# Up projection of an encoder block: hi-hi and hi-lo matmuls joined into one of 512 columns, relu squared on ScalarE, a weight sum by DMA

## The chip, the cores and the metric

The kernel runs on one core of a Trainium2 chip. The metric is the device time of one execution in microseconds (us). One execution of it was also taken with the hardware profiler; all rows below are from that one.

## The reference

One layer of an encoder block over 512 tokens of width 2048, all in float32:

```
h = rmsnorm(x) ; p = h @ w_in                      # 2048 x 6144
mix = concat(8 differential heads, 8 neighbourhood heads)
x = x + mix @ w_out
u = rmsnorm(x) @ w_up                              # 512 x 2048 @ 2048 x 8192
x = x + square(relu(u)) @ w_down                   # 8192 x 2048
y = rmsnorm(x)
```

The change is in the product with `w_up` and in the relu squared behind it.

## The kernel before

TensorE multiplies tiles of type float32r. To keep float32 accuracy each operand is split in two: a high part (a cast on ScalarE, L94, to a tile `wh`) and the rest (a subtraction on VectorE, L95, to a tile `wl`). A product of two split operands is three matmuls: high by high, high by low, low by high.

The up projection cuts its matrices in halves both ways and uses Strassen-like sums, in the Winograd form: seven products in the place of eight. Seven sums of blocks of the activations (`a11`, `a12`, `s2`, `s1_`, `s3`, `s4`, `a22`; each split, each with its high and low part side by side in one tile) are made once. The loop `for q in range(32)` then takes 256 columns of `w_up` a turn. Its four weight blocks (128 x 1024 each, 512 KB) are loaded by the SP queue into the pool `rx` (6 buffers), in the order b11, b12, b22, b21. The generator `quad` makes from them the seven weight operands, in this order: b11, b21, t2 = t1 + b22, t1 = b11 + b12, t3 = b12 + b22, b22, t4 = t2 + b21. The sums are VectorE additions (L471) into the pool tag `raw` (3 buffers); each operand is split into a `wh` and a `wl` tile, and each of these two tags has three buffers. This work is queued with raised priority, some way ahead of the products. The activations are the moving side (256 tokens), the weights the stationary one.

`prod` (L593) runs one product: 8 k-tiles by 3 matmuls of 256 columns, 24 matmuls. Three PSUM banks hold the results of a turn: pU gets a11, then s2, s3 and a22 on top of it; pV gets a12; pW gets s1_, then s4. Between the products that add to pU or pW the value so far is taken out: ScalarE keeps copies p1 (after a11), u2 (after s2) and p5 (after s1_), and VectorE combines them with later values into four quarters of a tile `c` (L605, L611, L613; the fourth is a ScalarE copy, L615). A product that adds to a bank waits for the copy that reads it. L617 makes relu squared of the whole of `c` in one VectorE pass, and GpSimd's queue writes it to DRAM (`ud`), from where the down projection (L776) reads it.

The order of the instructions on each engine is set when the program is built, by a list scheduler with priorities; at run time every engine takes its own instructions strictly in that order. A tile of a pool is given out again when its last reader is done.

The down projection already has transfers that add to a tile in SBUF (L681, `accum_op=ALU.add`), issued by GpSimd's queue.

Of the kernel before, what the change touches and what calls it, by code (L numbers as in the profile page):

```python
# [9 lines left out]
F32 = mybir.dt.float32  # L10
F32R = mybir.dt.float32r
AF = mybir.ActivationFunctionType
ALU = mybir.AluOpType
AX = mybir.AxisListType

P = 128
# [19 lines left out]
def hymba_kernel(ctx: ExitStack, tc: tile.TileContext, x, x_t, norm_mix_g, w_dq, w_dk, w_dv, w_nq, w_nk, w_nv, lams,  # L36
                 subln_g, rel_bias, w_out, norm_mlp_g, w_up, w_down, norm_final_g, cos_t, sin_t, mask_t, out):
    nc = tc.nc
# [54 lines left out]
    def split(hi, lo, src, eng=None):  # L93
        nc.scalar.copy(out=hi, in_=src)  # L94
        (eng or nc.vector).tensor_sub(out=lo, in0=src, in1=hi.bitcast(F32))  # L95
# [55 lines left out]
    with tc.tile_pool(name="start", bufs=4) as sp, tc.high_priority(offset=20000):  # L151
        acc = sp.tile([P, 2 * SEQ], F32, name="acc", bufs=1)
        xs = []
        for u in range(4):
# [8 lines left out]
            for k in range(4):  # L163
# [3 lines left out]
                                               op0=ALU.mult, op1=ALU.subtract)  # L167
# [14 lines left out]
        for t in range(NT):  # L182
            nc.tensor.matmul(out=ssx[:, t:t + 1], lhsT=acc[:, t * P:(t + 1) * P], rhs=ones_f[:, 0:1],
                             start=True, stop=True)
# [11 lines left out]
    with es:  # L196
# [19 lines left out]
        with tc.issue_after(last_sq.ins):  # L216
            for r in range(GH):
                src = bass.AP(rel_bias.tensor, rel_bias.offset + 15 * 15 + 7 - r, [[TD * 15, NH], [-15, 16], [1, TRUN]])
# [187 lines left out]
        for hp in range(NH // 2):  # L406
# [5 lines left out]
            last = hp == NH // 2 - 1  # L412
# [14 lines left out]
    stage = up_es.enter_context(tc.tile_pool(name="stage", bufs=2))  # L427
# [34 lines left out]
    def quad(src, pool_t):  # L462

        with tc.high_priority(offset=3000):
            b11, b12, b22, b21 = (rx.tile([P, 1024], F32, name="b", tag="b") for _ in range(4))
            for t, i in ((b11, 0), (b12, 1), (b22, 3), (b21, 2)):
                nc.sync.dma_start(out=t, in_=src[i])

            def add(a, b):
                t = pool_t.tile([P, 1024], F32, name="ts", tag="raw")  # L470
                nc.vector.tensor_add(out=t, in0=a, in1=b)  # L471
                return t

            def parts(t):
                h = wpool.tile([P, 1024], F32R, name="wh", tag="wh")
                l = wpool.tile([P, 1024], F32R, name="wl", tag="wl")
                split(h, l, t)
                return h.rearrange("p (k c) -> p k c", k=8), l.rearrange("p (k c) -> p k c", k=8)

            t1 = add(b11, b12)  # L480
            yield parts(b11)
            t2 = add(t1, b22)
            yield parts(b21)
            yield parts(t2)
            yield parts(t1)
            t3 = add(b12, b22)
            yield parts(t3)
            yield parts(b22)
            t4 = add(t2, b21)
            yield parts(t4)  # L490
# [8 lines left out]
    with tc.tile_pool(name="trans", bufs=2) as tr:  # L499
        for n in range(4):  # L500
# [7 lines left out]
            for u in range(8):  # L508
# [3 lines left out]
                for t in range(NT):  # L512
                    ts = slice(t * P, (t + 1) * P)
                    for k in range(2):
                        kt = 2 * u + k
                        m = mixT[kt // 4]
# [10 lines left out]
            for th in range(2):  # L527
# [3 lines left out]
                for t in (2 * th, 2 * th + 1):  # L531
                    xt = tr.tile([P, 512], F32, name="xg", tag="xg", bufs=3)
                    nc.vector.scalar_tensor_tensor(out=xt, in0=xb[t], scalar=s1[:, t:t + 1], in1=gM, op0=ALU.mult,
                                                   op1=ALU.mult)
                    xg.append(xt)
                for k2 in range(2):
                    pt = ((psa,) * 4, (psb, psc) * 2)[n % 2][2 * th + k2]().rearrange("p (k t) -> p k t", k=2)
                    for k in range(2):
                        for i in range(2):
                            nc.tensor.transpose(out=pt[:, k, i * P:(i + 1) * P],  # L540
                                                in_=xg[i][:, (2 * k2 + k) * P:(2 * k2 + k + 1) * P], identity=ident)
# [13 lines left out]
    def psm():  # L555
        return psM.tile([P, 512], F32, name="pm", tag="pm")
# [27 lines left out]

    for q in range(32):
        ops = quad(w_up[q], wpool)
        pU, pV, pW = (psm()[:, :256] for _ in range(3))

        def prod(ps, s, first, last):
            th_, tl_ = next(ops)  # L590
            for k in range(8):
                for i, (a, j) in enumerate(((th_, 0), (th_, 1), (tl_, 0))):
                    nc.tensor.matmul(out=ps, lhsT=a[:, k], rhs=s[k // 4][:, j, k % 4], start=first and k + i == 0,  # L593
                                     stop=last and k == 7 and i == 2, skip_group_check=True)

        def keep_copy(ps, name):
            t = stage.tile([P, 256], F32, name=name, tag=name)
            nc.scalar.copy(out=t, in_=ps)  # L598
            return t

        c = stage.tile([P, 2, 2, 256], F32, name="c", tag="c")
        prod(pU, a11, True, True)
        p1 = keep_copy(pU, "p1")
        prod(pV, a12, True, True)
        nc.vector.tensor_add(out=c[:, 0, 0], in0=pV, in1=p1)  # L605
        prod(pU, s2, False, True)
        u2 = keep_copy(pU, "u2")
        prod(pW, s1_, True, True)
        p5 = keep_copy(pW, "p5")
        prod(pU, s3, False, True)  # L610
        nc.vector.scalar_tensor_tensor(out=c[:, 1, 1], in0=pU, scalar=-1.0, in1=p5, op0=ALU.mult, op1=ALU.subtract)  # L611
        prod(pW, s4, False, True)
        nc.vector.scalar_tensor_tensor(out=c[:, 1, 0], in0=pW, scalar=-1.0, in1=u2, op0=ALU.mult, op1=ALU.subtract)  # L613
        prod(pU, a22, False, True)
        nc.scalar.copy(out=c[:, 0, 1], in_=pU)  # L615
        cf = c.rearrange("p m h t -> p (m h t)")
        nc.vector.scalar_tensor_tensor(out=cf, in0=cf, scalar=0.0, in1=cf, op0=ALU.max, op1=ALU.mult)  # L617
        nc.gpsimd.dma_start(out=ud[q], in_=cf)


# [184 lines left out]
    for p in range(16):  # L805
        c, n = divmod(p, 2)
        o = chunks[c]
        pU, pW = X[p % 2], X[1 - p % 2]
        end = p == 15
# [36 lines left out]
        for b in range(2):  # L846
            t = 2 + b
# [3 lines left out]
                                           op1=ALU.add)  # L851
# [87 lines left out]
```

## Time and profile before

| | |
|---|---|
| median of 3 runs | 2127.74 us (2125.85 to 2128.14) |
| the profiled execution | 2128.14 us; span from first to last instruction 2126.0 us |
| busy: TensorE matmuls | 2080.7 us (98%), 12604 matmuls |
| busy: weight loads of TensorE | 1853.7 us (87%) |
| busy: VectorE, ScalarE, GpSimd | 1527.0 us (72%), 982.5 us (46%), 282.6 us (13%) |
| granted clock of TensorE, mean | 0.993 of full speed |
| up projection, L593 | 5376 matmuls between 841.7 and 1482.7 us |

Matmuls overlap one another, so the length shown for one is not its cost; the distance between the starts of two is. A row of the timeline is: start in us, length in us, engine, line, operation, output <- inputs, shape, count, and in brackets the idle time before it with what ended it. Names are the program's without buffer numbers: `pm` is any of the three banks, `a` any of a11, a12 and a22, `s` any of s2, s3 and s4 (s1_ shows as s__7304), `p` is p1 or p5, `ts` any of t1 to t4.

### The profile page before, as it was taken

What the parts mean: (1) busy time and instruction counts of PE and PEld (TensorE: products, weight loads), DVE (VectorE), ACT (ScalarE), POOL (GpSimd) and SP (SyncE); (2) the same over time, 40 slices, a digit from 0 to 9 for tenths busy, and PEclk for the clock granted to TensorE, in tenths of its full rate; (3) what the DMA queues carried; (4) which work ended last, traced back from release to release, by engine and by line L of the source; (5) the groups of instructions that cost most, each with busy time, mean ns of one, the idle gap of its engine ahead of it and who ended that gap; (6) DMA issues with size and microseconds to landing.
All of it is one profiled execution on the core that took longest, in us unless ns stands there. A gap on an engine that the chain in (4) does not pass through costs nothing.

```text
span 2126.0 us, 31142 instructions
## 1 busy us (share of the span) xinstructions
PE 2080.7 (98%) x12604; PEld 1853.7 (87%) x12604; DVE 1527.0 (72%) x1707; ACT 982.5 (46%) x1342; POOL 282.6 (13%) x271
## 2 busy tenths in 40 slices
PE   7999999999999999999999999999999999999996
PEld 6989989989888887999999999999888878788875
DVE  6656556556566345877777877778777788788788
ACT  5444444444445434444444444444554555445544
POOL 5221221221221000000000000000011111111110
PEclk8999999999999999999999999999999999999998
DMA  6322332332324642634334434335888798798873
GB/s 217 114 95 89 109 97 88 108 98 85 105 92 136 223 156 87 209 129 149 129 119 150 141 128 139 131 129 178 226 223 216 178 243 217 190 246 211 214 182 109
DMA packets 109552, 323.51 MB, mean 152 GB/s; under 512 B 11296, under 2 KB 27872, under 8 KB 109408
## 3 DMA queue, kind: packets, MB, share of 16 engines
q1 hardware_dynamic: 83040, 241.33, 34.0%
q0 software_dynamic: 25936, 79.65, 16.7%
q8 instruction: 99, 1.62, 0.3%
q10 hardware_dynamic: 432, 0.53, 0.1%
q14 instruction: 45, 0.37, 0.1%
HBM read 275.33 MB, written 30.25 MB: 144 GB/s over the span
## 4 chain that ended last, share of the span: by engine, by line
PE 81%; DVE 8%; DMA 5%; issue 2%; ACT 2%; POOL 0%; SPq 0%; ACTq 0%; DVEq 0%; POOLq 0%
PE pm L593 28%; PE x L776 13%; PE pa L141 8%; PE pa L98 7%; PE pa L99 7%; PE pa L100 7%; DMA b<-in_w_down 5%; DVE wl L95 3%; PE v L776 2%; PE pb L99 1%; PE pb L98 1%; PE pb L100 1%; DVE b L685 1%; PE pc L98 1%; PE pc L99 1%
## 5 line engine op out<-in xcount | busy, mean ns | idle before, releaser
L94 ACT CAST wh<-b 128x1024 fp32r<-128x1024 f32 x320 | 333.3, 1049 | 452.9 <-PE x L776 156.2
L776 PE MATMUL x<-wh,uT 128*128 128x512 f32 x1536 | 482.0, 392 | 8.7 <-DVE y L790 7.8
L95 DVE TENSOR_TENSOR wl<-b,wh 128x1024 fp32r<-128x1024 f32 x320 | 388.3, 1220 | 115.8 <-ACT wh L94 114.2
L776 PEld LDWEIGHTS x<-wh,uT 128*128 128x128 f32 x1536 | 288.8, 188 | 76.5 <-issue 4.5
L776 PE MATMUL x<-wl,uT 128*128 128x512 f32 x768 | 301.2, 392 | 0.9 <-DVE wl L95 0.9
L593 PE MATMUL pm<-s,wh 128*128 128x256 f32 x1536 | 280.2, 283 | 3.4 <-ACT p L598 2.3
L593 PE MATMUL pm<-a,wh 128*128 128x256 f32 x1536 | 267.3, 279 | 2.0 <-DVE c L611 1.4
L593 PEld LDWEIGHTS pm<-s,wh 128*128 128x128 f32 x1536 | 239.4, 192 | 4.0 <-ACT p L598 2.8
L593 PEld LDWEIGHTS pm<-a,wh 128*128 128x128 f32 x1536 | 232.8, 189 | 2.4 <-DVE c L611 1.6
L95 DVE TENSOR_TENSOR wl<-ts,wh 128x1024 fp32r<-128x1024 f32 x128 | 154.8, 1222 | 105.7 <-ACT wh L94 104.2
L89 ACT CAST wh<-raw 128x1024 fp32r<-128x1024 f32 (+1 forms) x129 | 134.5, 1043 | 200.3 <-PE pa L99 72.1
L593 PE MATMUL pm<-s,wl 128*128 128x256 f32 x768 | 217.9, 284 | 1.6 <-DVE wl L95 1.6
L94 ACT CAST wh<-ts 128x1024 fp32r<-128x1024 f32 x128 | 132.6, 1051 | 186.9 <-PE pm L593 165.7
L141 PE MATMUL pa<-wh,hT 128*128 128x256 f32 x1024 | 201.2, 291 | 14.1 <-DVE hT L166 7.9
L593 PE MATMUL pm<-a,wl 128*128 128x256 f32 x768 | 209.5, 278 | 0.0
L90 DVE TENSOR_TENSOR wl<-raw,wh 128x1024 fp32r<-128x1024 f32 (+1 forms) x98 | 121.0, 1235 | 117.7 <-ACT wh L89 116.1
L100 PE MATMUL pa<-hT,wl 128*128 128x512 f32 x512 | 201.3, 393 | 0.0
L99 PE MATMUL pa<-hT,wh 128*128 128x512 f32 x512 | 200.9, 392 | 0.0
L98 PE MATMUL pa<-hT,wh 128*128 128x512 f32 x512 | 200.7, 392 | 0.0
L141 PEld LDWEIGHTS pa<-wh,hT 128*128 128x128 f32 x1024 | 168.2, 197 | 18.9 <-DVE hT L166 9.3
L776 PEld LDWEIGHTS x<-wl,uT 128*128 128x128 f32 x768 | 144.5, 188 | 33.1 <-DVE wl L95 2.2
L593 PEld LDWEIGHTS pm<-s,wl 128*128 128x128 f32 x768 | 147.2, 192 | 2.0 <-DVE wl L95 2.0
(250 smaller groups left out, 3576.4 us busy)
## 6 DMA issues: line engine op xcount, KB each, us to landing
b<-in_w_down SPq DMA_DIRECT2D x130, 512.0 KB, 6.4
b<-in_w_up SPq DMA_DIRECT2D x128, 512.0 KB, 3.7
b<-in_w_down POOLq DMA_DIRECT2D x64, 512.0 KB, 10.2
raw<-in_w_out SPq DMA_DIRECT2D x32, 512.0 KB, 3.4
ud<-c POOLq DMA_DIRECT2D x32, 512.0 KB, 3.1
ur<-ud SPq DMA_DIRECT2D x32, 512.0 KB, 9.3
y<-st POOLq DMA_DIRECT2D x26, 512.0 KB, 11.1
raw<-in_w_dq SPq DMA_DIRECT2D x16, 512.0 KB, 3.4
```

The source lines that it names most:

```text
L89: nc.scalar.copy(out=wh[:, cs], in_=raw[:, cs])
L90: eng.tensor_sub(out=wl[:, cs], in0=raw[:, cs], in1=wh[:, cs].bitcast(F32))
L94: nc.scalar.copy(out=hi, in_=src)
L95: (eng or nc.vector).tensor_sub(out=lo, in0=src, in1=hi.bitcast(F32))
L98: nc.tensor.matmul(out=ps, lhsT=lh, rhs=rh, start=first, stop=False)
L99: nc.tensor.matmul(out=ps, lhsT=lh, rhs=rl, start=False, stop=False)
L100: nc.tensor.matmul(out=ps, lhsT=ll, rhs=rh, start=False, stop=last)
L141: nc.tensor.matmul(out=ps[t], lhsT=a, rhs=b[:, k, :], start=first and i == 0, stop=last and i == 2, skip_group_check=True)
L593: nc.tensor.matmul(out=ps, lhsT=a[:, k], rhs=s[k // 4][:, j, k % 4], start=first and k + i == 0, stop=last and k == 7 and i == 2, skip_gro ...
L685: nc.vector.tensor_add(out=a, in0=a, in1=b)
L776: m = nc.tensor.matmul(out=ps[:, b], lhsT=l, rhs=r[:, k], start=first and u + k + i == 0, stop=last and u == 1 and k == 1 and i == 2, skip ...
```

## The change

1. `prod` makes two matmuls of each three: high weights by the high and the low part of the activations together, 512 columns into a whole bank (its two halves), then low weights by the high part, 256 columns into the first half.
2. So every result is in two halves that have to be added. The copies are 512 wide, the combinations (`minus`) work on 512 columns in place, and `both` adds the halves into `c`, four times a turn. The kept copies have one buffer each in the place of two; the copy of a22 (`u4`) uses the tag of p1.
3. Relu squared is two ScalarE passes, a relu and a square.
4. t1 is made in the buffer of b11 by a transfer from DRAM that adds b12 to it, on GpSimd's queue, behind the split of b11; b12 is still loaded for t3.

```diff
@@ -477,8 +477,9 @@
                 split(h, l, t)
                 return h.rearrange("p (k c) -> p k c", k=8), l.rearrange("p (k c) -> p k c", k=8)
 
-            t1 = add(b11, b12)
             yield parts(b11)
+            t1 = b11
+            nc.gpsimd.dma_start(out=t1, in_=src[1], accum_op=ALU.add)
             t2 = add(t1, b22)
             yield parts(b21)
             yield parts(t2)
@@ -584,37 +585,52 @@
 
     for q in range(32):
         ops = quad(w_up[q], wpool)
-        pU, pV, pW = (psm()[:, :256] for _ in range(3))
+        pU, pV, pW = (psm().rearrange("p (j t) -> p j t", j=2) for _ in range(3))
 
         def prod(ps, s, first, last):
+
             th_, tl_ = next(ops)
             for k in range(8):
-                for i, (a, j) in enumerate(((th_, 0), (th_, 1), (tl_, 0))):
-                    nc.tensor.matmul(out=ps, lhsT=a[:, k], rhs=s[k // 4][:, j, k % 4], start=first and k + i == 0,
-                                     stop=last and k == 7 and i == 2, skip_group_check=True)
+                o, end = s[k // 4], last and k == 7
+                nc.tensor.matmul(out=ps, lhsT=th_[:, k], rhs=o[:, :, k % 4], start=first and k == 0, stop=False,
+                                 skip_group_check=True)
+                nc.tensor.matmul(out=ps[:, 0], lhsT=tl_[:, k], rhs=o[:, 0, k % 4], start=False, stop=end,
+                                 skip_group_check=True)
 
         def keep_copy(ps, name):
-            t = stage.tile([P, 256], F32, name=name, tag=name)
+            t = stage.tile([P, 2, 256], F32, name=name, tag=name, bufs=1)
             nc.scalar.copy(out=t, in_=ps)
             return t
 
+        def minus(ps, t):
+            nc.vector.scalar_tensor_tensor(out=t, in0=ps, scalar=-1.0, in1=t, op0=ALU.mult, op1=ALU.subtract)
+
         c = stage.tile([P, 2, 2, 256], F32, name="c", tag="c")
+
+        def both(m, h, t):
+            nc.vector.tensor_add(out=c[:, m, h], in0=t[:, 0], in1=t[:, 1])
+
         prod(pU, a11, True, True)
         p1 = keep_copy(pU, "p1")
         prod(pV, a12, True, True)
-        nc.vector.tensor_add(out=c[:, 0, 0], in0=pV, in1=p1)
+        nc.vector.tensor_add(out=p1, in0=pV, in1=p1)
+        both(0, 0, p1)
         prod(pU, s2, False, True)
         u2 = keep_copy(pU, "u2")
         prod(pW, s1_, True, True)
         p5 = keep_copy(pW, "p5")
         prod(pU, s3, False, True)
-        nc.vector.scalar_tensor_tensor(out=c[:, 1, 1], in0=pU, scalar=-1.0, in1=p5, op0=ALU.mult, op1=ALU.subtract)
+        minus(pU, p5)
+        both(1, 1, p5)
         prod(pW, s4, False, True)
-        nc.vector.scalar_tensor_tensor(out=c[:, 1, 0], in0=pW, scalar=-1.0, in1=u2, op0=ALU.mult, op1=ALU.subtract)
+        minus(pW, u2)
+        both(1, 0, u2)
         prod(pU, a22, False, True)
-        nc.scalar.copy(out=c[:, 0, 1], in_=pU)
+        u4 = keep_copy(pU, "p1")
+        both(0, 1, u4)
         cf = c.rearrange("p m h t -> p (m h t)")
-        nc.vector.scalar_tensor_tensor(out=cf, in0=cf, scalar=0.0, in1=cf, op0=ALU.max, op1=ALU.mult)
+        nc.scalar.activation(out=cf, in_=cf, func=AF.Relu)
+        nc.scalar.square(cf, cf)
         nc.gpsimd.dma_start(out=ud[q], in_=cf)
 
 
```

## Rows read from the trace of the kernel before

**Rows 1.** Window of busy time in the up projection (columns in the first row):

```profile
core 0: us, PE busy (x) PEld busy (x) DVE busy (x) ACT busy (x) POOL busy (x), PEclk, DMA share, GB/s
...
1000.00:1200.00 200.00, 200.00 (x1709) 200.00 (x1708) 153.56 (x154) 84.91 (x113) 5.31 (x10) 1.00 0.42 137
```

**Rows 2.** The chain that ended last, 872 to 1470 us: start, us, what:

```profile
872.39 592.41 PE pm L593 x5053
```

**Rows 3.** Timeline of all engines, one turn of the loop:

```profile
1119.82 0.40 PE L593 MATMUL pm<-s,wh 128*128 128x256 f32 x2
...
1119.94 1.05 ACT L94 CAST wh<-b 128x1024 fp32r<-128x1024 f32 x1 [1.53 <-issue]
...
1121.02 1.23 DVE L95 TENSOR_TENSOR wl<-b,wh 128x1024 fp32r<-128x1024 f32 x1
...
1122.28 1.46 SPq L467 DMA_DIRECT2D b<-in_w_up  x2
...
1122.70 0.64 PE L593 MATMUL pm<-a,wh 128*128 128x256 f32 x4
...
1125.43 0.39 PE L593 MATMUL pm<-a,wh 128*128 128x256 f32 x2
...
1127.70 0.28 PE L593 MATMUL pm<-a,wl 128*128 128x256 f32 x1
...
1127.90 1.05 ACT L94 CAST wh<-ts 128x1024 fp32r<-128x1024 f32 x1 [4.08 <-PE pm L593]
...
1128.86 0.36 ACT L598 COPY p<-pm 128x256 f32<-128x256 f32 x1
...
1128.98 1.22 DVE L95 TENSOR_TENSOR wl<-ts,wh 128x1024 fp32r<-128x1024 f32 x1 [3.90 <-ACT wh L94]
...
1130.68 0.40 PE L593 MATMUL pm<-a,wh 128*128 128x256 f32 x2
...
1131.03 0.39 PE L593 MATMUL pm<-s,wh 128*128 128x256 f32 x2
```

**Rows 4.** Timeline of TensorE in the output projection, 20 rounds of 3 matmuls:

```profile
806.12 0.39 PE L98 MATMUL pb<-wh,mixT 128*128 128x512 f32 x1
...
819.72 0.39 PE L98 MATMUL pb<-wh,mixT 128*128 128x512 f32 x1
```

**Rows 5.** The chain that ended last, whole execution, down projection:

```profile
1494.33 32.94 PE x L776 x144
```

**Rows 6.** Groups of instructions: busy us, mean ns | idle before:

```profile
L605 DVE TENSOR_TENSOR c<-pm,p 128x256 f32<-128x256 f32 x32 | 13.5, 422 | 14.9 <-PE pm L593 14.9
...
L320 ACT ACT_TABLE_LOAD x8 | 10.3, 1283 | 0.1
...
L94 ACT CAST pth<-pb 128x512 fp32r<-128x512 f32 x16 | 9.3, 585 | 14.0 <-PE pb L386 14.0
...
L178 ACT ACTIVATE sqx<-xt 128x1024 f32<-128x1024 f32 x7 | 7.3, 1047 | 0.0
...
L529 DVE TENSOR_TENSOR xb<-xb,pa 128x512 f32<-128x512 f32 x8 | 5.3, 681 | 1.1 <-DMA xb<-in_x 1.1
```

**Rows 7.** Timeline, VectorE and GpSimd, one turn earlier:

```profile
1113.87 1.22 DVE L617 SCALAR_TENSOR_TENSOR c<-c 128x1024 f32<-128x1024 f32 x1
...
1115.39 0.53 POOL L618 DMA_DIRECT2D ud<-c  x1 [24.74 <-DVE c L617]
```

**Rows 8.** All 64 instructions of L681, issue to landing:

```profile
DMA to landing us min/median/max: 5.2/10.2/15.3
```

**Rows 9.** DMA issues of the page: count, size, median us to landing:

```profile
b<-in_w_down SPq DMA_DIRECT2D x130, 512.0 KB, 6.4
b<-in_w_up SPq DMA_DIRECT2D x128, 512.0 KB, 3.7
...
ud<-c POOLq DMA_DIRECT2D x32, 512.0 KB, 3.1
```

**Rows 10.** The one instruction of L681 issued between 1630 and 1631 us:

```profile
DMA to landing us min/median/max: 5.5/5.5/5.5
```

## The prediction

> **What bounds the kernel now.** I read a window of busy time first, then the chain that ended last, then the timeline of one turn of the up projection's loop. Between 1000 and 1200 us TensorE is busy for all 200 us and its granted clock is full (1.00, that is 2.4 GHz), VectorE for 153.56 us and ScalarE for 84.91 [rows 1]. The chain says the same: 592.41 us in one piece, 5053 matmuls of L593 with nothing between them [rows 2]. So the stage is TensorE's. One matmul there costs 592.41 / 5053 = 117.24 ns, and a turn of the loop (7 products of 24 matmuls, 168) 19.70 us; 32 turns.
>
> The timeline of one turn shows what feeds it [rows 3]. Product s3 ends at 1119.82. At once (1119.94) ScalarE casts the next turn's first weight tile (b11), because `wh` has three buffers and s3 frees one; VectorE subtracts at 1121.02. The cast of t2, the sum of three tiles, is at 1127.90, its subtraction at 1128.98, and the product that wants it (s2) starts at 1131.03: the subtraction ends only 0.83 us before. Between s3's end and s2's start stand four products (s4, a22, a11, a12), 11.21 us. Today t1 and t2 are sums that VectorE forms well ahead, so nothing in those 11.21 us hangs on a transfer. The change puts one there.
>
> **The change, part by part.**
>
> *Matmuls.* For each of the 8 k of a product, three of 256 columns become one of 512 and one of 256. 512-column matmuls run at (819.72 − 806.12) / 60 = 226.7 ns in the output projection [rows 4] and at 32.94 / 144 = 228.8 in the down projection [rows 5]. Before: 3 × 117.24 = 351.7 ns. After: 226.7 + 117.2 = 343.9. Saved: 7.8 ns, times 32 × 7 × 8 = 1792 is 14.0 us. The bounds: where the moving tile is an `s` the 256 columns cost (1122.70 − 1119.82) / 24 = 120 ns, where it is an `a` (1127.70 − 1125.43) / 20 = 113.5 [rows 3]; all pairs priced by the first give 360 − 346.7 = 13.3 ns and 23.8 us, by the second 340.5 − 340.2 = 0.3 ns and 0.5 us. I take 14.0, since the stage's mean mixes both. A product becomes 8 × 343.9 = 2.75 us, a turn 19.26. The new 512 columns are read in two pieces of 256, which no row here shows; I add nothing for it. The Trainium skill (TensorE: Matmul & The Clock Gate, Back-to-back issue gap) speaks against the edit: it gives a warm matmul N / 2.4 plus 2.5 ns, so joining two would save only those 2.5 ns, by our count 4.5 us in all. The rows disagree: here a matmul of 256 costs 10.6 ns above 256 / 2.4, one of 512 13 above its own.
>
> *Evictions and relu².* VectorE loses the sum t1 and the max-times pass of L617, 1.22 us each (L617 in [rows 7]; t1 is a pass of the same size), and three evictions of 256 (0.42, L605 in [rows 6]); it gains three of 512 from PSUM (0.68, L529) and four adds of halves (256 columns, 0.42 again): 15.13 − 2.44 − 1.26 + 2.04 + 1.68 = 15.15 us a turn, where 15.13 is 153.56 / 200 × 19.70. ScalarE's four copies grow from 0.36 (1128.86 in [rows 3]) to 0.59 (512 from PSUM, pth in [rows 6]), and relu and square add two passes of 1024 at 1.05 (L178): 8.36 + 0.9 + 2.1 = 11.4 us of 19. Both engines stay under TensorE, so this costs nothing by itself. If relu and square each needed a table load (1.28, L320) ScalarE would be at 14.0, still hidden; no row shows a relu, so the bounds are 0 and 2.6 us a turn off the path.
>
> *The weight sum by DMA.* The transfer adds in place into b11, so it waits for both readers of b11; then t2 waits for it. From s3's end: cast starts 0.12 later, subtraction 1.20 later (both as in [rows 3]); VectorE to a GpSimd issue takes 1115.39 − 1113.87 = 1.52 from the start of the VectorE instruction [rows 7], so the issue is at 2.72. The kernel's other accumulating loads (L681, also 512 KB) land after 5.2 us at least and 10.2 in the median [rows 8], in a stage whose plain loads take 6.4 instead of 3.7 [rows 9]; one that was issued alone took 5.5 [rows 10]. The up projection moves little (DMA share 0.42 [rows 1]), so I take 5.5: landing at 8.22. Then t2's add 1.22 and a hop (9.49), cast to subtraction 1.08 (10.57), subtraction 1.22 (11.79). s2 can start 11.79 us after s3's end, where the four products now take 11.0. TensorE idles for 0.8 us.
>
> Around this loop a turn lasts 11.79 + 3 × 2.75 = 20.04 us: 0.34 more than the 19.70 of before, although every product is shorter. That is with nobody in the way. Three VectorE steps meet an engine that is 77% busy with 1.2 us instructions, where half an instruction's wait is 0.47; two ScalarE steps meet one that is now 60% busy. At random these waits would be 1.4 and 0.6; the weight work has priority and VectorE is often idle just then [rows 3], so I take half, 1.0. That gives 21.0 a turn, +1.34. Bounds: landing 5.2 and no wait, 0.04 more than before; landing 10.2, 5.0 more. Behind an add that waits in VectorE's queue stand the subtraction of b21 (for a12) and the evictions that TensorE waits for before it writes a bank again, so where the add is queued early, a late landing stops a12 too.
>
> *One buffer for p1.* The kept copy of a22 (u4) uses the tile of p1, which has one buffer now, so the next turn's copy of a11 waits for u4's add, and s2 waits for that copy. In the timeline a22 is what TensorE fills gaps with: its last three matmuls come after a12, from 1130.68 on, directly ahead of s2 [rows 3]. If they stay there, s2 follows after u4's copy 0.59, the add 0.42, p1's copy 0.59 and four hops of about 0.1 (0.12 from s3's end to a cast): 1.95 us idle, 19.26 + 1.95 = 21.2 a turn, +1.5. It runs beside the DMA's wait, not behind it.
>
> *Sum.* The profiled execution took 2128.14 us (span 2126.0), 0.4 above the median of the runs. Its continuous part holds 30 turns. 30 × 1.4 (between the two causes) = 42: 2170 us. TensorE's 14 us are inside the 20.04: four of seven products no longer set the time.
>
> **Rivals.**
>
> *A, the accumulating transfer sets the turn:* 30 × 1.34, 2168. For it: every step above but one is measured in place. Against it: the down projection uses the same transfers and its TensorE runs on for long pieces all the same (144 matmuls in one, [rows 5]), though with products twice as long. Chance 0.45.
>
> *B, the p1 buffer sets it:* 2173. For it: where a22 stands now. Against it: the order of TensorE's queue is made anew and may put a22 first. 0.20.
>
> *C, the landing is slower or the add blocks VectorE's queue:* landing 7.0 and one whole VectorE instruction of wait more than in A, 1.34 + 1.5 + 1.2 = 4.0 at the worst; half of the added 2.7 gives 2.7 a turn, 81 us, 2209. For it: the median of 10.2 [rows 8]. Against it: two of the plain loads that today start at 1122.28, beside the new issue, will wait for b11 and go later. 0.15.
>
> *D, faster:* the transfer is covered and only TensorE's saving is left: 2128.1 − 14.0 = 2114. It decides where landing plus waits stay under 11.0 − (11.79 − 5.5) = 4.7 us. For it: plain transfers of GpSimd land in 3.1 [rows 9]. Against it: no accumulating one landed under 5.2. The Trainium skill (DMA: Bandwidth & Descriptors, Anatomy of one DMA) gives GpSimd's transfers 2.0 us plus bytes / 436e3, which is an estimate of 3.2 us for these; the 3.1 agree, the 5.2 of the accumulating ones do not. 0.14.
>
> *E, gain and wait cancel:* landing near 5.2, no waits, 2128. 0.06.
>
> **How the numbers follow.** A and B, 0.65 of the chance, lie together at about 2170; their own range is 2140 to 2195 (waits of 0.4 to 2.2 a turn). About 0.2% of the time, 4.3 us, is what a measurement can tell from no change. Slower: A, B, C, 0.80. Same: E, 0.06. Faster: D, 0.14. The range leaves out most of D (0.12) and the far end of C (0.07): 2119 to 2215.
>
> **What would show it.** The 512-column matmuls of L593 at 225 to 230 ns apart. TensorE idle once a turn, 1 to 2.5 us, ahead of s2, put down to the cast or subtraction of t2 or to a p1 copy, and `b` from w_up on GpSimd's queue at 5 to 7 us in the chain; turns of 20.5 to 21.5 us. VectorE's busy time a turn unchanged. I am wrong if the stage still shows one unbroken run of L593: then the transfer lands under 4.7 us or the cast of b11 comes before s3's end. A product longer than 2.75 us would show the two-piece read to have a price.

## The result, and the profile after

The median is 2206.21 us (4 runs, 2202.92 to 2214.84) beside 2127.94 for the kernel before on the same chip (4 runs): slower by 78 us where 42 was forecast. The ratio, formed over the runs and not from the two medians, is 1.0376 [1.0358, 1.0394]. The time lies inside the stated range, near its upper end. The profiled execution took 2202.92 us, its span 2201.1, which is 75.1 more than before.

The line numbers behind the diff have moved: the 512-column matmul is L595, the 256-column one L597, the DMA that sums L482, `minus` L606, `both` L611, the copies L602, relu and square L632 and L633.

First the windows of busy time of the kernel after, in the stage (columns: window, its length, busy us and count of TensorE, weight loads, VectorE, ScalarE, GpSimd, then the granted clock, the DMA share and GB/s), to be read against [rows 1]:

```profile
880.00:900.00 20.00, 13.43 (x63) 10.77 (x62) 12.45 (x13) 7.06 (x8) 1.71 (x2) 0.83 0.87 274
...
1000.00:1200.00 200.00, 189.62 (x1040) 158.93 (x1039) 139.38 (x157) 102.88 (x122) 13.24 (x19) 1.00 0.56 149
1200.00:1400.00 200.00, 188.80 (x1026) 158.12 (x1025) 138.26 (x156) 101.34 (x119) 12.66 (x18) 0.99 0.55 145
```

TensorE is no longer busy throughout: 189.62 us of 200, at a full granted clock (2.4 GHz). A turn is now 112 matmuls, so it takes 400 / 2066 × 112 = 21.68 us in the mean of the two later windows, where it took 19.66 by the same view (200 / 1709 × 168). That is 2.02 a turn in these windows. Counted by the starts of the stage's matmuls, the third turn begins at 903.5 us where it began at 889.2 before, 14.2 us late, and the last matmul of the stage starts at 1560.9 where it started at 1482.7, 78.1 late. So the 30 turns from the third on cost 63.9 us, 2.13 each, and the first two turns 14.2; 3 us are made up behind the stage.

Where the steady 2 us go shows in the timeline of one turn of the kernel after, the counterpart of [rows 3] (start, length, engine, line, operation; in brackets the idle time before it with what ended it). The first matmul of s4 starts at 1114.85; as in the prediction, this is taken for the end of s3:

```profile
1114.93 1.05 ACT L94 CAST wh<-b 128x1024 fp32r<-128x1024 f32 x1 [1.28 <-PE pm L595]
...
1116.19 1.22 DVE L95 TENSOR_TENSOR wl<-b,wh 128x1024 fp32r<-128x1024 f32 x1
...
1117.70 0.85 POOL L482 DMA_DIRECT2D b<-in_w_up  x1 [8.46 <-DVE wl L95]
...
1123.42 2.36 DVE L471 TENSOR_TENSOR ts<-b 128x1024 f32<-128x1024 f32 x2 [3.25 <-DMA b<-in_w_up]
...
1124.73 1.06 ACT L94 CAST wh<-ts 128x1024 fp32r<-128x1024 f32 x1 [3.23 <-DVE ts L471]
...
1125.70 0.42 DVE L611 TENSOR_TENSOR c<-p 128x256 f32<-128x256 f32 x1
...
1126.03 1.22 DVE L471 TENSOR_TENSOR ts<-ts,b 128x1024 f32<-128x1024 f32 x1
...
1126.78 0.49 PE L595 MATMUL pm<-s__7304,wh 128*128 128x512 f32 x1 [0.50 <-ACT wh L94]
...
1127.17 1.22 DVE L95 TENSOR_TENSOR wl<-ts,wh 128x1024 fp32r<-128x1024 f32 x1
...
1128.44 0.39 PE L597 MATMUL pm<-s,wl 128*128 128x256 f32 x1 [0.68 <-DVE wl L95]
```

It is the loop of the prediction, step by step: s3's end frees a buffer, b11 is cast (+0.08) and subtracted (+1.34), GpSimd issues (+2.85), the sum lands and t2 is added (+8.57), t2 is cast (+9.88) and subtracted (+12.32), and TensorE runs on at +13.59, after two 512-column matmuls that it could begin a little earlier. VectorE stands idle for 3.25 us ahead of the t2 addition, although the stage is short of time.

The waits of the kernel after from 900 to 1500 us (us in total, times, longest) name the same links:

```profile
POOL b L482 <- DVE wl L95: 246.0, 28, 14.9
...
DVE ts L471 <- DMA b<-in_w_up: 91.0, 28, 4.2
ACT wh L94 <- DVE ts L471: 90.5, 28, 4.2
...
PEld pm L597 <- DVE wl L95: 26.7, 27, 1.0
PEld pm L595 <- ACT wh L94: 23.0, 28, 1.8
```

TensorE itself meets only short waits, one or two in each turn, which a reader who looks at TensorE alone would put down to VectorE or ScalarE. The transfer stands three links earlier. By the page's table of DMA issues (count, size, median us to landing) it lands after 5.6 us:

```profile
b<-in_w_up POOLq DMA_DIRECT2D x32, 512.0 KB, 5.6
```

The landing varies from turn to turn, and the turn follows it. The distance between two issues is one turn; GpSimd's timeline shows two of them, and below stand the times to landing of the issue at 1271.15 and of the one at 1379.02:

```profile
1271.15 0.84 POOL L482 DMA_DIRECT2D b<-in_w_up  x1 [8.42 <-DVE wl L95]
1292.41 0.85 POOL L482 DMA_DIRECT2D b<-in_w_up  x1 [8.46 <-DVE wl L95]
...
1379.02 0.85 POOL L482 DMA_DIRECT2D b<-in_w_up  x1 [8.42 <-DVE wl L95]
1401.64 0.84 POOL L482 DMA_DIRECT2D b<-in_w_up  x1 [8.46 <-DVE wl L95]
...
DMA to landing us min/median/max: 5.3/5.3/5.3
...
DMA to landing us min/median/max: 6.6/6.6/6.6
```

The landings differ by 1.3 us and the turns, 21.26 and 22.62, by 1.36. From the third turn on this holds in 25 of the 29 distances: the turn is the landing plus 15.95 to 16.00 us. Three others, which begin at 965.0, 1204.5 and 1401.6, take 1.5 us more, and one 0.3; in the three TensorE's granted clock falls after the wait ahead of s2 (0.57 as the mean of 976 to 980, where 0.50 is 1.2 GHz). Why it falls in these turns and not in the others with the same wait is not shown.

The early loss has two places. In the first turn the t2 addition stands in VectorE's queue ahead of the last evictions of the output projection (L530). It waits 5.95 us for the transfer, and TensorE's transposes behind those evictions (L541) wait with it:

```profile
835.09 2.36 DVE L471 TENSOR_TENSOR ts<-b 128x1024 f32<-128x1024 f32 x2 [5.95 <-DMA b<-in_w_up]
...
838.50 0.68 DVE L530 TENSOR_TENSOR xb<-xb,pb 128x512 f32<-128x512 f32 x1
...
842.23 0.48 PE L541 MATMUL pb<-ident,xg 128*128 128x128 f32 x1 [4.55 <-DVE xg L534]
```

So the stage's first matmul starts at 848.0 us and not at 841.7. The kernels below whose transfer goes into b11 (2, 6 to 9) start the stage at 846.7 to 850.3, the others at 839.7 to 842.0. In the second turn, which takes 29.0 us where it took 20.0, the transfer is issued beside the first loads of `w_down` (DMA share 0.87 in the first row of the windows) and takes 10.6 us. The timelines of GpSimd and of TensorE in the kernel after show its issue and what TensorE pays:

```profile
873.04 0.89 POOL L482 DMA_DIRECT2D b<-in_w_up  x1 [29.44 <-DVE wl L95]
...
886.00 0.80 PE L595 MATMUL pm<-s,wh 128*128 128x512 f32 x1 [5.84 <-ACT wh L94]
```

With these 5.84 us of idle TensorE's granted clock falls (0.83 as the mean of 880 to 900): it is 0.50, that is 1.2 GHz, between 886 and 890 and 1.00 again between 895 and 900.

### The profile page after: what moved, and what is told of

The parts are those of the page before. It is cut to its first block, busy times and chain, and to the rows that moved or that the text cites. A ratio compares the mean times of both kernels' runs of the same rounds, so it can differ in the third digit from the quotient of the medians.

```text
span 2201.1 us, 27767 instructions
## 1 busy us (share of the span) xinstructions
PE 2114.3 (96%) x10812; PEld 1779.3 (81%) x10812; DVE 1528.2 (69%) x1771; ACT 1071.7 (49%) x1406; POOL 310.6 (14%) x303
## 5 line engine op out<-in xcount | busy, mean ns | idle before, releaser
L94 ACT CAST wh<-b 128x1024 fp32r<-128x1024 f32 x352 | 366.9, 1048 | 434.3 <-PE x L792 165.0
L95 DVE TENSOR_TENSOR wl<-b,wh 128x1024 fp32r<-128x1024 f32 x352 | 427.2, 1219 | 129.0 <-ACT wh L94 128.8
L595 PE MATMUL pm<-s,wh 128*128 128x512 f32 x768 | 285.2, 409 | 9.2 <-ACT wh L94 5.8
L595 PE MATMUL pm<-a,wh 128*128 128x512 f32 x768 | 271.9, 399 | 1.8 <-DVE p L606 1.8
L597 PE MATMUL pm<-s,wl 128*128 128x256 f32 x768 | 222.4, 290 | 20.8 <-DVE wl L95 20.8
L597 PE MATMUL pm<-a,wl 128*128 128x256 f32 x768 | 211.7, 282 | 0.0
L595 PEld LDWEIGHTS pm<-s,wh 128*128 128x128 f32 x768 | 147.8, 193 | 52.5 <-ACT p L602 11.3
L597 PEld LDWEIGHTS pm<-s,wl 128*128 128x128 f32 x768 | 148.7, 194 | 30.8 <-DVE wl L95 30.7
L595 PEld LDWEIGHTS pm<-a,wh 128*128 128x128 f32 x768 | 143.6, 190 | 34.4 <-DVE p L606 2.1
L94 ACT CAST wh<-ts 128x1024 fp32r<-128x1024 f32 x96 | 100.5, 1047 | 137.9 <-DVE ts L471 102.8
L471 DVE TENSOR_TENSOR ts<-b 128x1024 f32<-128x1024 f32 x64 | 75.6, 1222 | 105.2 <-DMA b<-in_w_up 105.2
```

Of the source, the lines that this page charges most:

```text
L595: nc.tensor.matmul(out=ps, lhsT=th_[:, k], rhs=o[:, :, k % 4], start=first and k == 0, stop=False, skip_group_check=True)
L597: nc.tensor.matmul(out=ps[:, 0], lhsT=tl_[:, k], rhs=o[:, 0, k % 4], start=False, stop=end, skip_group_check=True)
```

## The experiments

Each ratio is to the kernel before, run on the same chip.

**1. The change without the transfer.** t1 is a VectorE addition again; all else as after.

```diff
+            t1 = add(b11, b12)
             yield parts(b11)
-            t1 = b11
-            nc.gpsimd.dma_start(out=t1, in_=src[1], accum_op=ALU.add)
```

> The changed kernel with t1 as a VectorE addition again, everything else as changed. If the loop through the accumulating transfer makes the stall: TensorE runs unbroken, a turn is 56 pairs at 353 ns = 19.77 us, and the time is 2125 to 2140 us. If the halves, the wider evictions, the single buffer of p1 or the two ScalarE passes make it: the time stays at 2180 to 2206 us, with TensorE waiting for ScalarE or VectorE.

2133.19 us (10 runs), 1.0031 [1.0014, 1.0049]: 73 us come back. The window of this kernel:

```profile
1000.00:1200.00 200.00, 200.00 (x1137) 174.03 (x1137) 165.90 (x183) 113.61 (x133) 5.32 (x10) 1.00 0.46 135
```

TensorE is unbroken, so the count prices the joined matmuls cleanly: 200 / 1137 × 2 = 351.8 ns for a pair of 512 and 256 columns. Three of 256 took 200 / 1709 × 3 = 351.1. The 14 us that the joining was forecast to save are not there.

**2. The transfer alone.** The kernel before with the same three lines changed the other way round.

> The kernel before with the weight sum by DMA and nothing else. If the loop through the transfer makes the stall: chain of 11.8 us plus some 1.4 us of queueing from the end of s3 to the start of s2, plus three products of 2.81 us, about 21.6 a turn, 2185 to 2210 us. If the other parts make it: 2125 to 2140 us.

2184.84 us, 1.0278 [1.0245, 1.0311]: 57 us from the transfer by itself, in a kernel that still has the 256-column matmuls, two buffers for p1 and relu squared on VectorE. Its window, and one turn of VectorE and the TensorE instruction that follows it (of the turn before) in its timelines:

```profile
1000.00:1200.00 200.00, 189.82 (x1601) 187.89 (x1600) 132.84 (x132) 79.44 (x105) 14.12 (x20) 1.00 0.54 151
```

```profile
1101.86 0.39 PE L594 MATMUL pm<-s,wl 128*128 128x256 f32 x1 [1.08 <-DVE wl L95]
...
1118.04 2.36 DVE L471 TENSOR_TENSOR ts<-b 128x1024 f32<-128x1024 f32 x2 [2.57 <-DMA b<-in_w_up]
1120.32 1.21 DVE L471 TENSOR_TENSOR ts<-ts,b 128x1024 f32<-128x1024 f32 x1
1121.46 1.21 DVE L95 TENSOR_TENSOR wl<-ts,wh 128x1024 fp32r<-128x1024 f32 x1
```

A turn is 200 / 1601 × 168 = 20.99 us in this window. The same loop, and the same place in VectorE's queue: the t2 addition, then two more additions (t3 and t4), and only then t2's subtraction, 3.42 us after the addition began.

**3. The 512 columns in one piece.** Kernel 1, with the operand's tile laid out so that a matmul reads its 512 columns contiguously.

```diff
-        t = pool.tile([P, 2, 2, 4, 256], F32R, name=name, tag=tag)
-        return [t[:, 0], t[:, 1]]
+        t = pool.tile([P, 2, 4, 2, 256], F32R, name=name, tag=tag)
+        return [t[:, i].rearrange("p k h c -> p h k c") for i in range(2)]
```

> As e1, and the high and low parts of an activation block lie side by side, so that the 512 columns are read in one piece. If the read in two pieces is what takes the gain of the joined matmul: 512 columns at 227 to 229 ns apart, a pair at 344 to 346 and not 353, 12 to 16 us less than e1, about 2115 us. If a pair costs 353 in any layout (a price of 512 beside 256 columns): the same as e1.

2129.89 us (10 runs), 1.0016 [1.0002, 1.0030], and again 1137 matmuls in 200 us. The two-piece read is not what holds the pair at 352 ns.

**4. The sum into b12, early.** t3 is formed first, which frees b12; the transfer adds b11 into b12 and no longer waits for the split of b11.

```diff
+            t3 = add(b12, b22)
+            t1 = b12
+            nc.gpsimd.dma_start(out=t1, in_=src[0], accum_op=ALU.add)
             yield parts(b11)
-            t1 = b11
-            nc.gpsimd.dma_start(out=t1, in_=src[1], accum_op=ALU.add)
...
-            t3 = add(b12, b22)
```

> The changed kernel, but the transfer adds b11 into b12 (t3 is summed first), so that it doesn't wait for the split of b11 and can start a dozen us earlier. Same transfers, same bytes. If the place of the transfer in the loop makes the stall: the stall goes, 2125 to 2145 us. If the transfer as such does (its load on the DMA engines or on GpSimd's queue): 2180 us or more remains.

2150.42 us, 1.0108 [1.0078, 1.0137]: between the two forecasts. 56 of the 78 us are gone, with the transfer still there; a turn is 20.3 us (1103 matmuls between 1000 and 1200). The transfer is issued at 1118.20, behind the t3 addition (1116.16 to 1117.38; the row names a later ScalarE copy as what released it), some 13 us earlier in the turn than in the kernel after. It lands after 7.3 us in the median, so the t2 addition is at 1125.69, well ahead of the turn that uses it, which begins at 1133.9. Part of what is left is what stands behind that addition in VectorE's queue: a subtraction comes late, and TensorE waits for it at 1128.10.

```profile
1116.16 1.22 DVE L471 TENSOR_TENSOR ts<-b 128x1024 f32<-128x1024 f32 x1
...
1118.20 0.85 POOL L482 DMA_DIRECT2D b<-in_w_up  x1 [18.01 <-ACT p L602]
...
1125.69 1.23 DVE L471 TENSOR_TENSOR ts<-b 128x1024 f32<-128x1024 f32 x1 [3.72 <-DMA b<-in_w_up]
1126.83 1.22 DVE L95 TENSOR_TENSOR wl<-b,wh 128x1024 fp32r<-128x1024 f32 x1
...
1128.10 0.39 PE L597 MATMUL pm<-s,wl 128*128 128x256 f32 x1 [0.33 <-DVE wl L95]
```

**5. The matmuls grouped.** Kernel 1, with the eight 512-column matmuls of a product first and then the eight of 256.

```diff
                                  skip_group_check=True)
+            for k in range(8):
+                o, end = s[k // 4], last and k == 7
                 nc.tensor.matmul(out=ps[:, 0], lhsT=tl_[:, k], rhs=o[:, 0, k % 4], start=False, stop=end,
```

> As e1 (no transfer sum), and within a product the eight matmuls of 512 columns come first, then the eight of 256. e1 and e3 showed a pair at 352 ns in either layout, the 512 columns at 235. If the price comes from the alternation of the two lengths: 512 columns at 227 ns back to back, a pair at 341 to 345, 13 to 18 us less than e1, about 2117 us. If 512 columns of these operands cost 235 in any order: within 4 us of e1, about 2133.

2157.89 us, 1.0144 [1.0127, 1.0161]. Where nothing stops TensorE, mean distances between starts give 347 to 349 ns a pair (512 columns at 229 to 233, 256 at 114 to 119), against 234 to 236 and 117 to 118 in kernel 1: some 3 ns less, not 8. Neither forecast was met: the gain is lost to new waits. Two that kernel 1 does not have, from this kernel's table of waits from 900 to 1500 us:

```profile
DVE wl L95 <- PE pm L598: 74.5, 29, 2.7
...
PE pm L594 <- ACT p L603: 22.1, 30, 1.7
```

**6. t3's addition ahead of t2's.** The kernel after, with `t3 = add(b12, b22)` moved up two lines, so that t2's subtraction no longer stands behind it.

> The changed kernel, with t3's addition written ahead of t2's, so that it no longer stands in VectorE's queue between t2's addition and t2's subtraction. If the order behind the transfer's wait is a part of the stall: one addition (1.1 us a turn) less, 30 turns, some 33 us, 2170 to 2180 us. If the stall is the transfer alone or something else: no change, 2200 to 2210.

2203.10 us, 1.0358 [1.0332, 1.0385]: no gain. t2's subtraction did move up, to 2.61 us behind its addition (1121.81 to 1124.42, was 3.75). But the first matmul that TensorE has in its queue there is one of s1_, with t1's high part, and ScalarE casts t1 after t2 and a relu. The timelines of ScalarE and TensorE in this kernel:

```profile
1123.12 1.05 ACT L94 CAST wh<-ts 128x1024 fp32r<-128x1024 f32 x1 [3.06 <-DVE ts L471]
1124.08 1.05 ACT L632 ACTIVATE c<-c 128x1024 f32<-128x1024 f32 x1
1125.04 1.03 ACT L94 CAST wh<-b 128x1024 fp32r<-128x1024 f32 x1
...
1126.12 0.50 PE L595 MATMUL pm<-s__7304,wh 128*128 128x512 f32 x1 [1.28 <-ACT wh L94]
```

**7. A plain transfer in place of the adding one.** The kernel after without `accum_op`: the sum t1 is left out, its buffer holds b12 alone; what waits for what stays.

> The changed kernel with a plain load into b11's buffer in the place of the adding one (t1 is then b12 alone: the sum is left out). If the landing of the accumulating transfer is on the loop: it lands in 3.1 to 3.7 us and not 5.6, some 2 us a turn less, so TensorE is nearly unbroken again: 2140 to 2160 us. If the stall comes from the order of the queues alone: less than 15 us of change.

2142.65 us, 1.0071 [1.0056, 1.0086]. The transfer now lands after 3.9 us in the median, 1.7 less, and TensorE is busy for all but 0.6 us of the same window:

```profile
1000.00:1200.00 200.00, 199.38 (x1125) 171.32 (x1125) 151.27 (x170) 111.59 (x131) 10.66 (x20) 1.00 0.50 158
```

With the 1131 matmuls from 1200 to 1400 a turn is 400 / 2256 × 112 = 19.86, 1.8 shorter than after for a landing that is 1.7 earlier: the landing stands on the loop, microsecond for microsecond. Turn by turn, landings of 3.74 us and more again give the landing plus 15.95, with one exception, while the shortest, 3.62 to 3.69, leave the turn at 19.7 (one at 20.0), TensorE's own time in kernel 1. So the landing comes off the loop at about 3.75 us.

**8. A buffer of its own for u4.** The kernel after, with `u4 = keep_copy(pU, "p5")` in place of `"p1"`.

> The changed kernel with the copy of a22 in the buffer of p5 (free since s3) and not of p1. If the single buffer of p1 holds s2 up: 30 turns of 0.3 to 1.5 us less, 2160 to 2196 us. If the transfer's loop sets the start of s2: 2200 to 2210 us, no change.

2204.83 us, 1.0370 [1.0344, 1.0396]: nothing changes. The one buffer of p1 is not on the path.

**9. t3 and t4 added on GpSimd.** The kernel after, with these two additions given to GpSimd, to clear VectorE's queue.

> The changed kernel with the additions t3 and t4 on GpSimd, so that nothing of them stands behind the transfer's wait in VectorE's queue. If VectorE's queue behind the wait is a part of the stall, as e6 was to show before TensorE's own order hid it: the subtraction of t2 follows its addition by 2.4 us and not 3.75, some 1.3 us a turn less, about 2165 us. If landing alone counts: 2195 to 2210 us.

2207.68 us, 1.0373 [1.0344, 1.0401]: no gain. TensorE again waits for the cast of t1 (1.29 us at 1127.37), with a relu ahead of it on ScalarE. And the VectorE instructions beside a GpSimd addition become longer, as the timelines of the two engines show:

```profile
1118.08 2.71 POOL L471 TENSOR_TENSOR ts<-b 128x1024 f32<-128x1024 f32 x1
...
1118.41 2.68 DVE L611 TENSOR_TENSOR c<-u 128x256 f32<-128x256 f32 x1
...
1124.42 2.45 POOL L471 TENSOR_TENSOR ts<-ts,b 128x1024 f32<-128x1024 f32 x1 [3.63 <-DVE ts L471]
...
1125.45 2.50 DVE L95 TENSOR_TENSOR wl<-ts,wh 128x1024 fp32r<-128x1024 f32 x1 [0.83 <-ACT wh L94]
```

**10. Every matmul of 512 columns.** Kernel 1, with the low weights multiplied by both halves as well. This adds the product low by low, a third more columns, and is meant only for the price of a 512-column matmul beside others of its kind.

> As e1, but the low weights are multiplied by both halves too (low by low added, 512 columns in place of 256: a third more columns). If 512 columns cost 227 ns when no 256 stands between: a pair at 454 ns, the stage 1792 times 102 ns, 183 us, longer than e1, about 2316 us. If 512 columns of these operands cost 235 in any company: a pair at 470 ns, about 2345 us.

2367.47 us in one run, over both forecasts: TensorE also waits here, about 1 us a turn, so only distances within unbroken products are read. In the timeline of TensorE one product of an `s` begins at 1101.47, and two `a` matmuls stand at:

```profile
1101.47 0.40 PE L594 MATMUL pm<-s,wh 128*128 128x512 f32 x1
...
1112.38 0.39 PE L594 MATMUL pm<-a,wh 128*128 128x512 f32 x1
...
1117.04 0.39 PE L594 MATMUL pm<-a,wh 128*128 128x512 f32 x1
```

Three products of `s`, 48 matmuls, take 10.91 us, 227.3 ns each; 20 of `a` take 4.66, 233; `s1_` stays at 233 to 235. So 227 exists in this stage too, but for one operand alone and in this company; beside 256-column matmuls it was not seen.

**11. Relu and square alone.** The kernel before, with its last VectorE pass replaced by the two ScalarE passes.

> The kernel before with relu squared as two ScalarE passes and nothing else. If, as predicted, this costs nothing by itself: 2122 to 2132 us, no table loads in the up projection. If ScalarE's queue delays casts: TensorE waits in the stage, over 2135 us.

2125.33 us (10 runs), 0.9987 [0.9973, 1.0001]: no difference that can be told, with TensorE unbroken (1709 matmuls in 200 us) and no table load in the stage.

**12. The joined matmuls alone.** Kernel 1, with relu squared back in one VectorE pass.

> The joined matmuls, the wider evictions and the adds of the halves alone (relu squared on VectorE, t1 by VectorE). If a pair costs what the three cost, as e1 shows, and VectorE's work of 16.4 us a turn still hides under TensorE's 19.7: 2126 to 2136 us. If VectorE without the relief of the ScalarE passes is too late: TensorE waits for subtractions, 2140 us and more.

2227.15 us, 1.0460 [1.0435, 1.0485]: the second forecast, and far beyond its 2140. One VectorE pass of 1.22 us a turn in the place of two on ScalarE costs 94 us against kernel 1. It is not a lack of VectorE time, as the window of this kernel shows, and its waits from 900 to 1500 us name a ring:

```profile
1000.00:1200.00 200.00, 177.55 (x982) 150.09 (x980) 151.32 (x167) 81.03 (x96) 4.26 (x8) 1.00 0.36 111
```

```profile
DVE wl L95 <- PE pm L596: 88.1, 26, 3.7
...
PE pm L594 <- ACT p L601: 40.6, 27, 1.5
PEld pm L596 <- DVE wl L95: 35.3, 26, 1.7
```

VectorE is busy for 151 of 200 us, less than the 166 of kernel 1. But once a turn it stands, up to 3.7 us, at a subtraction whose `wl` buffer TensorE has not freed, with other work queued behind; then TensorE waits for VectorE and for a ScalarE copy. Kernel 1 has no such wait of VectorE for TensorE. The orders of the queues are made anew at each build, so the likely cause is where this build put that subtraction; an order changed by hand with all else kept was not tried, so this is argued, not shown.

## Why the prediction was right, and where it was off

**What bounds the kernel** held: kernel 1 and experiment 11 are again unbroken TensorE runs, about 0.3% above and 0.1% below the kernel before.

**The weight sum by DMA** was named as the main cause, and the runs bear it out. With it alone 57 us appear (2); without it 73 of 78 go (1); with a transfer that lands 1.7 us earlier the turn shortens by 1.8 (7); with one that starts from another buffer 56 us go (4). That is rival A. The turns say it most plainly: each is its own landing plus 15.95 to 16.00 us, where the prediction's loop is its landing plus 20.04 − 5.5 + 1.0 = 15.54. Its steps were close: cast 0.08 (0.12), subtraction 1.34 (1.20), issue 2.85 (2.72), issue to t2's addition 5.72 (5.5). The term that was too small is the waits in the queues. 1.0 was allowed; in the turn shown it is 13.59 − 11.79 = 1.80, and 1.40 of that is one place: from t2's addition to t2's subtraction 3.75 us instead of 2.35, because t3's addition, a sum of halves and t4's addition stand between them on VectorE. This is the queue of rival C, at a smaller price. It isn't a cost that can be removed by itself: with the additions out of the way, the cast of t1 behind a relu takes its place (6, 9).

The turn then follows: 13.59 and three products of 8 × 0.352 = 2.82 make 22.04, less the two 512-column matmuls that start early (0.5), 21.5, where the windows give 21.5 and 21.8. The forecast was 21.0: 0.8 more for waits and 0.2 for longer products, 0.5 less for the early start.

**Matmuls** was the wrong step. 343.9 ns was forecast for a pair, 14 us less in all; the pair takes 351.8, and nothing is saved. The 226.7 of [rows 4] was measured beside other 512-column matmuls and with other operands, and it did not carry over: beside a 256 the 512 takes 234 to 236. Joining does save on `s`, where three of 256 took 358.6 as the mean distance of their starts, but on `a` (347) and `s1_` (343) it loses as much. The lower bound, 0.5 us, was the nearer end. The sign that was given for a price of the two-piece read, a product longer than 2.75 us, did appear (2.82), but experiment 3 shows that the read is not its cause. The Trainium skill (TensorE: Matmul & The Clock Gate, Back-to-back issue gap) gives N / 2.4 + 2.5 ns as the gap of a single matmul by itself, a condition that the prediction left out; for a stream of weight loads and matmuls it says that both set the spacing, and gives about 131 ns for 512 columns. These runs agree with neither: 227 to 236 ns for 512 columns, and 0.7 ns more per k, where the formula gives an estimate of 2.5 less. What sets 227 or 235 is open: the layout of the operand is excluded (3), and grouping recovers 3 of the 8 ns (5).

**Evictions and relu squared** cost at most the 0.3% of kernel 1 where the edits come together, and relu squared alone nothing that can be told (11). VectorE's busy time is (139.38 + 138.26) / 400 × 21.68 = 15.05 us a turn (forecast 15.15), ScalarE's 11.1 (11.4). But the reason given, that both engines stay under TensorE, was not enough: with the joined matmuls and relu squared on VectorE (12) both stay under TensorE as well and 99 us are lost. The parts do not add: joined matmuls with ScalarE's relu +0.3%, the same without it +4.6%, the transfer alone +2.8%, all together +3.8%.

**One buffer for p1** (rival B) was wrong: experiment 8 takes it away and nothing moves.

**The sum.** 42 us were 30 turns of 1.4. Measured are 30 turns of 2.13, 64 us, and 14 in the first two turns, less 3 behind the stage. The 14 the prediction left out: it took the landing of a quiet stretch for all turns, and the second turn's took 10.6 us; it named the add that is queued early and holds up what stands behind it, but gave that no price, and in the first turn it delayed the stage by 6.3 us.

So the time lies outside the 2140 to 2195 that were given to A and B, and next to the 2209 of C, whose slow landing of 7.0 did not come. What was right is the mechanism; that a range of 96 us holds the time says little more, and its closeness to C's number is luck. Rival D needs a landing under about 3.75 us (7), which no adding transfer in these runs reached (5.1 at the least, in experiment 2); the plain one at 3.9 comes close to covering itself, and still is not faster than before.

No kernel here is faster than before by more than can be measured; relu and square on ScalarE alone comes nearest, 2125.33 us, and its interval includes no change.

## What to carry to other kernels

Before an addition moves from an engine to a transfer, follow the ring of buffers: from the instruction that frees the destination, through issue, landing and every conversion, to the instruction that needs the result, and compare that length with the work that stands between the two. If the ring is longer, each microsecond of landing is paid in each turn, and the busy shares won't show it; a destination that is free early (experiment 4) buys most of it back. Look also at the first turn, where other work stands in the queue behind the instruction that waits for the transfer. Price a matmul of another width from the same operands in the same company before counting on a few per cent, and look at the waits anew after any edit that rebuilds the static orders: in experiment 12 a small edit lost 94 us to them (that the order is the cause is argued there, not shown).

## What was not expected of the hardware

- A 512-column float32r matmul takes 227 to 236 ns and one of 256 columns 113.5 to 120, at a full granted clock, by operand and by what stands beside it; one by one the values are in experiments 5 and 10 and in [rows 3].
- The adding transfer of 512 KB lands 1.7 us later than a plain one at the same place in the same queue (5.6 and 3.9, medians of 32). The Trainium skill (DMA: Bandwidth & Descriptors, Anatomy of one DMA), whose figures gave the estimate of 3.2, is nearer to the plain one and has the adding one far too early.
- A VectorE instruction with two SBUF inputs that meets an addition on GpSimd ended only after it in experiment 9, in 29 sums of halves (0.29 us after) and 31 subtractions (1.08 us after). In the rows shown, GpSimd's first ends at 1118.08 + 2.71 = 1120.79 and VectorE's, begun at 1118.41, at 1121.09, 2.68 us for what takes 0.42 elsewhere. The Trainium skill (SBUF — State Buffer, Who interferes with whom) says that a VectorE instruction with two SBUF inputs contends with a GpSimd one that reads SBUF; these rows agree.
